# One inference step of a streaming encoder: the last piece of the down projection in the plain form

## The chip, the cores and the metric

The kernel runs on one core of one Trainium2 chip. A core has five engines that run their own instruction streams and meet at semaphores: TensorE (PE, matrix products into PSUM; PEld is its weight load), VectorE (DVE), ScalarE (ACT), GpSimd (POOL, here only issuing DMAs) and SyncE (SP, which issues the other DMAs). The metric is device microseconds of the whole program, the median of repeated runs; lower is better. The weights come from HBM by DMA, everything else is worked on in SBUF (128 partitions) and PSUM (eight banks of 128 x 512 floats).

## The reference

One layer is computed for 384 rows (256 of a new stream, 8 x 16 of running ones). The change lies in the MLP, at its end:

```
hdn = square(relu(rmsnorm(x, g_mlp_pre) @ w_up)) @ w_down     # 2048 -> 8192 -> 2048
x   = x + rmsnorm(hdn, g_mlp_post)
```

All matrices are float32. Ahead of the MLP stand the input projection, a pooling branch, a state-space branch and two output projections; the change does not touch them.

## The kernel before, in words

**Products.** A float32 product is made of three matmuls on operands split in two: a high part `h` (rounded to the PE's fast 32-bit type by ACT, an ACTIVATE with Copy) and a low part `l` (the rest, a DVE subtraction). h·h, h·l and l·h are added up in PSUM. So each weight unit of 128 x 1024 goes through three steps before PE may use it: a 512 KB load on SP's queue into a `w` buffer (`wfetch`, L65), ACT's `wh` (L72), DVE's `wl` (L73). `wpool` has three buffers of each of `w`, `wh`, `wl`; a buffer is handed out again when its last reader is done, so a load waits for an earlier unit's DVE split, and an ACT split waits for PE to be through with an earlier unit.

**Up projection.** `up(f)` makes tile f of 64 (128 of the 8192 hidden columns for all 384 rows) from two weight units, 24 matmuls of 384 columns each, then relu and square (ACT). Two tiles make a pair `R`. `combine(p)` turns pair p into ten 128 x 128 blocks `hh`/`hl`: five raw blocks (H11, H31, H22, H12, H32) and five sums (S1 to S4, H3). The first block of a pair, H21, is used in sums only.

**Down projection.** It runs in eight stretches `c` of 1024 hidden columns, each in two pieces `sb` of 1024 output columns. The first two row blocks (b = 0, 1), the two hidden tiles of a pair and the two 512-column halves of a piece form 2 x 2 blocks and use a seven-product Strassen form; the third row block (b = 2) is done plainly. `blocks(c, sb, w)` runs one piece: eleven groups of twelve matmuls of 512 columns, 132 in all, in the order a, c, b, d, e, f, g. Its weights are four quadrants of 1 MB from `w_dn`, loaded by POOL's queue in `prep`, and three sums of them that DVE makes (`add`, L1312: six halves of 128 x 1024 by the three steps `adds[0]`, `adds[1]`, `adds[2]`), plus one sum inside `blocks`. Every quadrant half is split by ACT (L1345) and DVE (L1346) as above. Products for b = 0, 1 go from PSUM into `acc` by `evict` (L1368); those for b = 2 stay in four banks `c3` until the end.

**Order.** The program is written in one stream; a scheduler places each instruction on its engine by priority and by what is free in its own model. `up(f, steps, steps)` runs its extra steps behind its first and second weight unit; a piece's `adds` are spread over the up tiles that follow its `prep`.

**End.** After `blocks(7, 0)` no up tiles are left: `prep(7, 1)`, its three sums at once, `blocks(7, 1)`. `tally(b, nb, src)` finishes a 512-column block: ACT squares and sums it (L1297), DVE multiplies it by the norm weights `gpo` (L1298); with the fourth block of a row block it makes the norm factor (`postnorm`, L978 to L986, then L1302), scales and adds the residual `x1` (four L1305) and stores (L1308, SP). `x1` (3 MB) and `gpo` (1 MB, scaled by ACT at L1450) are loaded after the last up tile, `x1` by SP, `gpo` by POOL.

Of the kernel before, what the change touches and what calls it, by code (L numbers as in the profile page):

```python
# [6 lines left out]
F32 = mybir.dt.float32  # L7
# [7 lines left out]
P = 128  # L15
# [18 lines left out]
def build(ctx, tc, io):  # L34
# [17 lines left out]
    def mmtile(name):  # L52
        return psm.tile([P, 512], F32, tag="mm", name=name)
# [4 lines left out]
    def behind(ins):  # L58
        return nullcontext() if ins is None else tc.issue_after(ins.ins)
# [1181 lines left out]
    with ExitStack() as mlp:  # L1241
# [25 lines left out]

        HB = {}

        def combine(p):  # L1270
# [21 lines left out]
        def tally(b, nb, src):  # L1292
            dst = end["z"][:, blk(nb)] if b == 2 else acc[:, b, blk(nb)]
            q = end["pool"].tile([P, 512], F32, tag="q3", name=f"q3_{nb}_{b}", bufs=2)
            i = count[b]
            count[b] += 1
            s.activation(q, src, AF.Square, scale=rr[:, b : b + 1], accum_out=end["st"][:, b, i : i + 1])  # L1297
            v.tensor_tensor(dst, src, end["gpo"][:, blk(nb)], ALU.mult)  # L1298
            if i < 3:
                return  # L1300
            y = postnorm(end["pool"], end["st"], b, "n3", doubled=True)
            v.tensor_tensor(y, y, rr[:, b : b + 1], ALU.mult)  # L1302
            for i in range(4):
                z = end["z"][:, blk(i)] if b == 2 else acc[:, b, blk(i)]
                v.scalar_tensor_tensor(  # L1305
                    out=z, in0=z, scalar=y, in1=end["x1"][:, b, blk(i)], op0=ALU.mult, op1=ALU.add
                )
                sy.dma_start(io["y"][b][:, blk(i)], z)  # L1308

        def add(out, a, b):  # L1310
# [276 lines left out]
```

## Time and profile before

| what | us |
|---|---|
| median of 3 runs (lowest, highest) | 2640.62 (2639.19, 2641.0) |
| the profiled execution's own time | 2640.17 |
| its span on the core | 2638.3 |
| PE busy, share of the span | 2607.0, 99% |
| DVE busy, share | 1791.4, 68% |
| ACT busy, share | 1308.0, 50% |

The span counts from the first to the last recorded instruction; 1.87 us lie around it. Rows of a timeline read: start, time, engine, line, operation, what is written and read, shape, and in brackets how long the engine stood idle before it and what ended that. A PE row's time reaches into the next one's, since matmuls are pipelined; what counts is the distance of two starts.

### The profile page before, as it was taken

How to read it: one execution, taken by the hardware profiler on the slowest of the kernel's cores; microseconds unless marked ns; L12 is line 12 of the kernel's file. 1: busy time of each engine (PE TensorE's matmuls, PEld its weight loads, DVE VectorE, ACT ScalarE, POOL GpSimd, SP SyncE). 2: the span in 40 equal slices, each digit the busy share in tenths (PEclk: the TensorE clock that was granted, in tenths of full speed). 3: DMA queues.
4: the chain of work that ended last, by engine and by line, in shares of the span. 5: the costliest groups of instructions: out<-in, count | busy, mean ns of one | idle time of the engine just before them, and what ended most of it. 6: DMA issues, size and time to landing. Idle time of an engine off the chain costs nothing.

```text
span 2638.3 us, 40306 instructions
## 1 busy us (share of the span) xinstructions
PE 2607.0 (99%) x15987; PEld 2506.8 (95%) x15987; DVE 1791.4 (68%) x2396; ACT 1308.0 (50%) x1983; POOL 186.3 (7%) x265
## 2 busy tenths in 40 slices
PE   9999999999999999999999999999999999999996
PEld 8999999999999999999999988999999999999995
DVE  6576334788887888876444435667686867767688
ACT  6443225566566666644333334655454544545453
POOL 0000000001110111120000000000000000000000
PEclk9999999999999999999999999999999999999998
DMA  7444445566666676666655455534344444434342
GB/s 275 141 139 152 146 148 205 185 201 207 231 210 220 205 235 199 233 209 233 193 164 161 153 189 180 184 129 143 128 153 159 144 137 144 143 128 144 128 168 96
DMA packets 138844, 457.76 MB, mean 174 GB/s; under 512 B 17504, under 2 KB 44704, under 8 KB 124704
## 3 DMA queue, kind: packets, MB, share of 16 engines
q1 hardware_dynamic: 116400, 325.93, 38.4%
q0 software_dynamic: 22256, 129.26, 13.4%
q8 instruction: 126, 2.06, 0.3%
q14 instruction: 62, 0.51, 0.1%
HBM read 410.26 MB, written 44.86 MB: 173 GB/s over the span
## 4 chain that ended last, share of the span: by engine, by line
PE 93%; issue 2%; DVE 2%; ACT 1%; DMA 1%; POOL 0%; DVEq 0%; POOLq 0%; ACTq 0%
PE pj_up L102 5%; PE pj_up L100 5%; PE pj_up L101 5%; PE pj_x L100 5%; PE pj_x L102 4%; PE pj_x L101 4%; PE pj_sp L101 3%; PE pj_z L102 3%; PE pj_z L101 3%; PE pj_z L100 3%; PE pj_sp L102 3%; PE pj_sp L100 3%; PE c L1360 2%; PE c L1361 2%; PE c L1359 2%
## 5 line engine op out<-in xcount | busy, mean ns | idle before, releaser
L102 PE MATMUL pj_up<-x1h,wl_up 128*128 128x384 f32 (+1 forms) x1024 | 333.8, 326 | 2.5 <-DVE wl_up L73 2.5
L100 PE MATMUL pj_up<-x1h,wh_up 128*128 128x384 f32 (+1 forms) x1024 | 333.9, 326 | 0.0
L101 PE MATMUL pj_up<-x1l,wh_up 128*128 128x384 f32 (+1 forms) x1024 | 333.7, 326 | 0.0
L100 PE MATMUL pj_x<-xgh,wh_x 128*128 128x384 f32 x768 | 252.0, 328 | 0.0
L102 PE MATMUL pj_x<-xgh,wl_x 128*128 128x384 f32 x768 | 250.6, 326 | 1.3 <-DVE wl_x L73 1.3
L101 PE MATMUL pj_x<-xgl,wh_x 128*128 128x384 f32 x768 | 250.4, 326 | 0.0
L72 ACT ACTIVATE wh_up<-w_up 128x1024 fp32r<-128x1024 f32 x126 | 133.1, 1056 | 189.3 <-PE pj_up L101 113.8
L102 PEld LDWEIGHTS pj_up<-x1h,wl_up 128*128 128x128 f32 x1024 | 193.5, 189 | 2.8 <-DVE wl_up L73 2.8
L73 DVE TENSOR_TENSOR wl_up<-w_up,wh_up 128x1024 fp32r<-128x1024 f32 x126 | 153.7, 1220 | 61.3 <-ACT wh_up L72 60.4
L101 PEld LDWEIGHTS pj_up<-x1l,wh_up 128*128 128x128 f32 x1024 | 193.5, 189 | 0.4
L100 PEld LDWEIGHTS pj_up<-x1h,wh_up 128*128 128x128 f32 x1024 | 193.5, 189 | 0.4
L101 PE MATMUL pj_z<-xgl,wh_z 128*128 128x384 f32 x512 | 166.9, 326 | 0.0
L102 PE MATMUL pj_z<-xgh,wl_z 128*128 128x384 f32 x512 | 166.9, 326 | 0.0
L100 PE MATMUL pj_sp<-abh,wh_sp 128*128 128x384 f32 x512 | 166.9, 326 | 0.0
L101 PE MATMUL pj_sp<-abl,wh_sp 128*128 128x384 f32 x512 | 166.9, 326 | 0.0
L102 PE MATMUL pj_sp<-abh,wl_sp 128*128 128x384 f32 x512 | 166.9, 326 | 0.0
L100 PE MATMUL pj_z<-xgh,wh_z 128*128 128x384 f32 x512 | 166.9, 326 | 0.0
L73 DVE TENSOR_TENSOR wl_sp<-w_sp,wh_sp 128x1024 fp32r<-128x1024 f32 x64 | 78.3, 1223 | 116.6 <-ACT wh_sp L72 116.6
L72 ACT ACTIVATE wh_x<-w_x 128x1024 fp32r<-128x1024 f32 x96 | 101.0, 1052 | 107.0 <-PE pj_z L101 53.0
L73 DVE TENSOR_TENSOR wl_x<-w_x,wh_x 128x1024 fp32r<-128x1024 f32 x96 | 117.3, 1222 | 52.3 <-ACT wh_x L72 52.3
L72 ACT ACTIVATE wh_sp<-w_sp 128x1024 fp32r<-128x1024 f32 x64 | 67.7, 1058 | 166.4 <-PE pj_sp L101 158.3
L100 PEld LDWEIGHTS pj_x<-xgh,wh_x 128*128 128x128 f32 x768 | 145.1, 189 | 2.6 <-issue 0.4
(409 smaller groups left out, 7133.9 us busy)
## 6 DMA issues: line engine op xcount, KB each, us to landing
w_up<-w_up SPq DMA_DIRECT2D x128, 512.0 KB, 3.5
w<-w_dn POOLq DMA_DIRECT2D x64, 1024.0 KB, 5.2
w_x<-w_in SPq DMA_DIRECT2D x96, 512.0 KB, 3.8
w_z<-w_in SPq DMA_DIRECT2D x64, 512.0 KB, 3.6
w_sp<-w_ssd SPq DMA_DIRECT2D x64, 512.0 KB, 3.5
w_ga<-w_ga SPq DMA_DIRECT2D x32, 512.0 KB, 3.5
w_pp<-w_pp SPq DMA_DIRECT2D x32, 512.0 KB, 3.5
hs<-ssm POOLq DMA_DIRECT2D x16, 1024.0 KB, 6.6
```

The source lines that it names most:

```text
L72: cut[0] = s.activation(h, w, AF.Copy)
L73: cut[1] = v.tensor_tensor(l, w, h.bitcast(F32), ALU.subtract)
L100: te.matmul(out, wh, xh, start=first, stop=False, **how)
L101: te.matmul(out, wh, xl, start=False, stop=False, **how)
L102: return te.matmul(out, wl, xh, start=False, stop=last, **how)
L1359: te.matmul(o, h[:, t], vh, start=go, stop=False, skip_group_check=True)
L1360: te.matmul(o, h[:, t], vl, start=False, stop=False, skip_group_check=True)
L1361: last[0] = te.matmul(o, l[:, t], vh, start=False, stop=False, skip_group_check=True)
```

## The change

**1.** The last piece (c = 7, sb = 1) is no longer `prep` and `blocks`. It is done plainly in two passes of 512 columns (nb = 2, 3), with all three row blocks, from a new input `w_tail` that holds these weights as eight units of 128 x 1024 (`kp` = 0 to 3 for each pass). Pass 2 runs unit by unit, 18 matmuls a unit. Pass 3 first has its four units split and kept (two in `wpool`, two in `t1` and `t2`, no longer needed for sums), and then runs row block by row block, 24 matmuls each, so that b = 0 and b = 1 are finished while b = 2 is still multiplied. The plain form needs H21: `combine` of the last four pairs also splits it, into a `w` buffer `h21` that is kept to the end. `tally` adds the finished PSUM block to `acc` (`add=True`) where before `evict` did.

**2.** At the start of the MLP the three `adds` of the first piece each run one up tile later.

**3.** The very last block (b = 2, nb = 3) is not multiplied by `gpo` ahead of the norm factor: when the factor is known, one instruction scales it out of PSUM by both, and one adds the residual.

**4.** `x1` is loaded on POOL's queue, behind `gpo`.

```
-        up(3, (), (adds[0],))
+        up(3)
         combine(1)
-        up(4, (adds[1],), (adds[2],))
-        up(5)
+        up(4, (), (adds[0],))
+        up(5, (adds[1],), (adds[2],))
...
-            sy.dma_start(x1[:, b, :], x1_scr[b])
+            gp.dma_start(x1[:, b, :], x1_scr[b])
         blocks(NC - 1, 0, w)
-        w, *adds = prep(NC - 1, 1)
-        for step in adds:
-            step()
-        blocks(NC - 1, 1, w)
+        for nb in (2, 3):
...
+            if nb == 2:
+                for kp in range(4):
+                    hl = wload(units[kp], names[kp])
+                    with behind(last[0]):
+                        for i in (2 * kp, 2 * kp + 1):
+                            for b in range(3):
+                                mm(b, hl, i)
+                for b in range(3):
+                    tally(b, nb, o[b], b < 2)
+                continue
+            w = []
+            for kp in range(4):
+                f_, name = wfetch(units[kp], names[kp])
+                if kp < 2:
+                    w.append(wsplit((f_, name)))
+                    continue
+                t = pr.tile([P, 2048], F32R, tag=f"t{kp - 1}", name=f"e_{name}")
+                h, l = t[:, :1024], t[:, 1024:]
+                s.activation(h, f_, AF.Copy)
+                v.tensor_tensor(l, f_, h.bitcast(F32), ALU.subtract)
+                w.append((h, l))
+            for b in range(3):
+                with behind(last[0]):
+                    for i in range(8):
+                        mm(b, w[i // 2], i)
+                tally(b, nb, o[b], b < 2)
```

In `tally` and `combine`:

```
+            if add:
+                v.tensor_tensor(dst, dst, src, ALU.add)
...
-            v.tensor_tensor(dst, src, end["gpo"][:, blk(nb)], ALU.mult)
+            g = end["gpo"][:, blk(nb)]
+            if i < 3 or b < 2:
+                v.tensor_tensor(dst, src, g, ALU.mult)
...
+                if b == 2 and i == nb:
+                    v.scalar_tensor_tensor(out=z, in0=src, scalar=y, in1=g, op0=ALU.mult, op1=ALU.mult)
+                    v.tensor_tensor(z, z, x, ALU.add)
...
+            if p < 4 * NC - 4:
+                return
+            if not extra:
+                extra.append(wpool.tile([P, 1024], F32R, tag="w", name="h21"))
+            i = p % 4 * 256
+            eh, el = extra[0][:, i : i + P], extra[0][:, i + P : i + 256]
+            s.activation(eh, R[:, :P], AF.Copy)
+            v.tensor_tensor(el, R[:, :P], eh.bitcast(F32), ALU.subtract)
```

**Where instructions move.** First place: DVE at the start of the MLP, in up tiles 4 and 5 (units 17029 and 17061 are tile 4, 17097 and 17127 tile 5; `t` and `w` rows are the sums, `hl` and `S` rows belong to `combine(1)`). Before:

```order
L73 TENSOR_TENSOR wl_up_0_17032<-w_up_0_17029,wh_up_0_17031 128x1024
L1312 TENSOR_TENSOR t_0_0_16950<-w_0_0_16942,w_0_0_16943 128x1024 x2
L73 TENSOR_TENSOR wl_up_1_17064<-w_up_1_17061,wh_up_1_17063 128x1024
L1312 TENSOR_TENSOR w_0_0_16943<-w_0_0_16943,w_0_0_16945 128x1024 x2
L1312 TENSOR_TENSOR t_0_0_16951<-t_0_0_16950,w_0_0_16945 128x1024 x2
L1277 TENSOR_TENSOR hl_17018<-R_16920,hh_17017 128x640
L1280 TENSOR_TENSOR S_17019<-R_16920 128x128
L1282 TENSOR_TENSOR S_17019<-R_16920 128x256
L1281 TENSOR_TENSOR S_17019<-S_17019,R_16920 128x128
L73 TENSOR_TENSOR wl_up_0_17100<-w_up_0_17097,wh_up_0_17099 128x1024
```

Now (tile 4 is 17027 and 17057, tile 5 is 17093 and 17125):

```order
L73 TENSOR_TENSOR wl_up_1_17060<-w_up_1_17057,wh_up_1_17059 128x1024
L1330 TENSOR_TENSOR t_0_0_16950<-w_0_0_16942,w_0_0_16943 128x1024 x2
L73 TENSOR_TENSOR wl_up_0_17096<-w_up_0_17093,wh_up_0_17095 128x1024
L1282 TENSOR_TENSOR S_17017<-R_16920 128x128
L1284 TENSOR_TENSOR S_17017<-R_16920 128x256
L1279 TENSOR_TENSOR hl_17016<-R_16920,hh_17015 128x640
L1283 TENSOR_TENSOR S_17017<-S_17017,R_16920 128x128
L1330 TENSOR_TENSOR w_0_0_16943<-w_0_0_16943,w_0_0_16945 128x1024
L1285 TENSOR_TENSOR S_17017<-S_17017,R_16920 128x128
L1330 TENSOR_TENSOR w_0_0_16943<-w_0_0_16943,w_0_0_16945 128x1024
L1287 TENSOR_TENSOR hl_17016<-S_17017,hh_17015 128x640
L73 TENSOR_TENSOR wl_up_1_17128<-w_up_1_17125,wh_up_1_17127 128x1024
```

The low part of tile 5's first unit stood behind all three sums and most of `combine(1)`; now it stands behind the first sum alone, and the second sum stands ahead of the low part of tile 5's second unit.

Second place: DVE at the handover from `blocks(7, 0)` to the last piece (`wl_g` is the last split of `blocks(7, 0)`, `Y_0` and `X_0` are its PSUM results). Before:

```order
L1346 TENSOR_TENSOR wl_g_0_1_24415<-t_7_0_23891,wh_g_0_1_24414 128x1024
L1312 TENSOR_TENSOR t_7_1_24436<-w_7_1_24428,w_7_1_24429 128x1024
L1298 TENSOR_TENSOR z_24205<-c_1_16928,gpo_24202 128x512
L1368 TENSOR_TENSOR acc<-acc,Y_0_24211 128x512
L1312 TENSOR_TENSOR t_7_1_24436<-w_7_1_24428,w_7_1_24429 128x1024
L1312 TENSOR_TENSOR w_7_1_24429<-w_7_1_24429,w_7_1_24431 128x1024
L1298 TENSOR_TENSOR acc<-acc,gpo_24202 128x512
L1368 TENSOR_TENSOR acc<-acc,X_0_24210 128x512
L1312 TENSOR_TENSOR w_7_1_24429<-w_7_1_24429,w_7_1_24431 128x1024
L1298 TENSOR_TENSOR acc<-acc,gpo_24202 128x512
L1312 TENSOR_TENSOR t_7_1_24437<-t_7_1_24436,w_7_1_24431 128x1024 x2
L1346 TENSOR_TENSOR wl_a_1_0_24448<-w_7_1_24428,wh_a_1_0_24447 128x1024
```

Now:

```order
L1364 TENSOR_TENSOR wl_g_0_1_24424<-t_7_0_23891,wh_g_0_1_24423 128x1024
L73 TENSOR_TENSOR wl_wt_0_24442<-w_wt_0_24439,wh_wt_0_24441 128x1024
L1313 TENSOR_TENSOR z_24214<-c_1_16928,gpo_24211 128x512
L1386 TENSOR_TENSOR acc<-acc,Y_0_24220 128x512
L73 TENSOR_TENSOR wl_wt_1_24466<-w_wt_1_24463,wh_wt_1_24465 128x1024
L1313 TENSOR_TENSOR acc<-acc,gpo_24211 128x512
L1386 TENSOR_TENSOR acc<-acc,X_0_24219 128x512
L73 TENSOR_TENSOR wl_wt_2_24490<-w_wt_2_24487,wh_wt_2_24489 128x1024
```

The six sum halves that stood between `wl_g` and the last piece's first low part are gone; the first unit's low part follows `wl_g` directly.

Third place: ACT in the last piece (`q_2_0` to `q_2_2` square the three blocks of pass 2, `e_wt_2` and `e_wt_3` are the high parts of the third and fourth unit of pass 3). Before, at the end of the last piece:

```order
L1345 ACTIVATE wh_g_1_1_24690<-t_7_1_24437 128x1024
L1297 ACTIVATE q_3_0_24596,st_24206<-acc,rr 128x512
L1297 ACTIVATE q_3_2_24631,st_24206<-c_3_16930,rr 128x512
L981 ACTIVATE n_n_24636<-st_24206,n_n_24634 128x1
L1297 ACTIVATE q_3_1_24656,st_24206<-acc,rr 128x512
L981 ACTIVATE n_n_24661<-st_24206,n_n_24659 128x1
L1297 ACTIVATE q_2_0_24701,st_24206<-acc,rr 128x512
L981 ACTIVATE n_n_24706<-st_24206,n_n_24704 128x1
```

Now:

```order
L1519 ACTIVATE e_wt_2_24562<-w_wt_2_24560 128x1024
L1310 ACTIVATE q_2_0_24536,st_24215<-acc,rr 128x512
L1310 ACTIVATE q_2_1_24540,st_24215<-acc,rr 128x512
L1310 ACTIVATE q_2_2_24543,st_24215<-c_2_16929,rr 128x512
L1519 ACTIVATE e_wt_3_24567<-w_wt_3_24565 128x1024
L1310 ACTIVATE q_3_0_24595,st_24215<-acc,rr 128x512
L981 ACTIVATE n_n_24600<-st_24215,n_n_24598 128x1
L1310 ACTIVATE q_3_1_24644,st_24215<-acc,rr 128x512
L981 ACTIVATE n_n_24649<-st_24215,n_n_24647 128x1
L1310 ACTIVATE q_3_2_24692,st_24215<-c_3_16930,rr 128x512
L981 ACTIVATE n_n_24696<-st_24215,n_n_24694 128x1
```

Before, three norm factors were made behind the last split, the last one for row block 0; now the third row block's comes last, and the high part of the fourth kept unit stands behind the three squares of pass 2.

More of the change, by code (lines that the diff above doesn't have):

```diff
@@ L1268, in build @@
         HB = {}
+        extra = []
         def combine(p):
@@ L1290, in build, with tally @@
         end = {}
-        def tally(b, nb, src):
+        def tally(b, nb, src, add=False):
             dst = end["z"][:, blk(nb)] if b == 2 else acc[:, b, blk(nb)]
+            if add:
+                v.tensor_tensor(dst, dst, src, ALU.add)
+                src = dst
             q = end["pool"].tile([P, 512], F32, tag="q3", name=f"q3_{nb}_{b}", bufs=2)
@@ L1304, in tally @@
                 z = end["z"][:, blk(i)] if b == 2 else acc[:, b, blk(i)]
-                v.scalar_tensor_tensor(
-                    out=z, in0=z, scalar=y, in1=end["x1"][:, b, blk(i)], op0=ALU.mult, op1=ALU.add
-                )
+                x = end["x1"][:, b, blk(i)]
+                if b == 2 and i == nb:
+                    v.scalar_tensor_tensor(out=z, in0=src, scalar=y, in1=g, op0=ALU.mult, op1=ALU.mult)
+                    v.tensor_tensor(z, z, x, ALU.add)
+                else:
+                    v.scalar_tensor_tensor(out=z, in0=z, scalar=y, in1=x, op0=ALU.mult, op1=ALU.add)
                 sy.dma_start(io["y"][b][:, blk(i)], z)
@@ new lines, in build, with mm @@
+        for nb in (2, 3):
+            o = [mmtile(f"wt{nb}_{b}") if nb == 2 else psd.tile([P, 512], F32, tag="XY"[b], name=f"wt{nb}_{b}") for b in range(2)]
+            o.append(c3[nb])
+            def mm(b, hl, i):
+                wh, wl = hl
+                mh, ml = lhs(i)[b]
+                q = slice(i % 2 * 512, i % 2 * 512 + 512)
+                out, vh, vl = pairs(o[b]), woven(wh[:, q]), woven(wl[:, q])
+                te.matmul(out, mh, vh, start=i == 0 and b < 2, stop=False, skip_group_check=True)
+                te.matmul(out, mh, vl, start=False, stop=False, skip_group_check=True)
+                last[0] = te.matmul(out, ml, vh, start=False, stop=False, skip_group_check=True)
+            names = [f"wt{nb}_{kp}" for kp in range(4)]
+            units = [io["w_tail"][nb - 2, kp] for kp in range(4)]
+            if nb == 2:
[24 more added lines that the diff above has]
+                tally(b, nb, o[b], b < 2)
@@ L1547 @@
         ).reshape(8, 2, 4, P, 2048),
+        "w_tail": _moving(np, a["w_down"][0][7168:, 1024:]),
         "state_pool": np.ascontiguousarray(a["state_pool"][0].reshape(NB, 15, KD, P).transpose(3, 2, 0, 1)),
```

5 lines of the change are left out of this document (added).

## The prediction

> **What bounds the kernel now.** I read the page first, then PE's waits from the last part of the program, then the stretches around them. On the page PE works for nearly the whole span; only the last of the forty slices is thin.
>
> ```profile
> span 2638.3 us, 40306 instructions
> ...
> PE 2607.0 (99%) x15987; PEld 2506.8 (95%) x15987; DVE 1791.4 (68%) x2396; ACT 1308.0 (50%) x1983; POOL 186.3 (7%) x265
> ...
> PE   9999999999999999999999999999999999999996
> ```
>
> So time can be won only where PE waits, or behind its last matmul. PE's waits from 1664 us to the end (engine and line that waited, what for, us, times, longest) are five:
>
> ```profile
> PE X L1360 <- DVE wl_a L1346: 4.7, 1, 4.7
> PE pj_up L102 <- DVE wl_up L73: 2.5, 1, 2.5
> PE c L1360 <- DVE wl_e L1346: 2.3, 3, 0.8
> PE c L1359 <- ACT wh_a L1345: 1.2, 1, 1.2
> PE X L1359 <- DVE acc L1368: 0.9, 1, 0.9
> ```
>
> The second is at the start of the MLP, the others in the last 60 us. Those I cut into four: the handover to the last piece, its first matmuls, the rest of them, and what follows the last matmul (bounds; length; busy time of PE, PEld, DVE, ACT, POOL with counts; granted clock; DMA share, GB/s).
>
> ```profile
> 2583.30:2591.20 7.90, 1.16 (x3) 0.37 (x2) 7.58 (x9) 3.10 (x6) 0.00 (x0) 0.74 0.00 0
> 2591.20:2597.40 6.20, 6.16 (x15) 4.91 (x16) 3.95 (x7) 1.06 (x1) 0.00 (x0) 0.51 0.00 0
> 2597.40:2624.00 26.60, 25.68 (x117) 21.53 (x115) 21.86 (x35) 13.44 (x21) 0.00 (x0) 1.00 0.00 1
> 2624.00:2638.30 14.30, 0.01 (x1) 0.00 (x0) 10.60 (x24) 1.11 (x3) 0.00 (x0) 0.64 0.59 220
> ```
>
> For 7.9 us PE does three matmuls while DVE is full; then fifteen run at a clock of 0.51; then it is full; then DVE alone works 10.6 of 14.3 us.
>
> **The sums one up tile later.** The early stall, on DVE and PE:
>
> ```profile
> 1684.56 1.22 DVE L73 TENSOR_TENSOR wl_up<-w_up,wh_up 128x1024 fp32r<-128x1024 f32 x1
> 1686.54 2.36 DVE L1312 TENSOR_TENSOR w<-w,w 128x1024 f32<-128x1024 f32 x2 [0.76 <-DVE wl_up L73]
> 1688.82 2.35 DVE L1312 TENSOR_TENSOR t<-t,w 128x1024 f32<-128x1024 f32 x2
> 1692.57 1.21 DVE L73 TENSOR_TENSOR wl_up<-w_up,wh_up 128x1024 fp32r<-128x1024 f32 x1
> ...
> 1693.83 0.43 PE L102 MATMUL pj_up<-x1h,wl_up 128*128 128x384 f32 x1 [2.47 <-DVE wl_up L73]
> ...
> 1694.00:1697.00 3.00, 3.00 (x19) 3.00 (x20) 2.98 (x3) 2.58 (x4) 0.00 (x0) 1.00 0.60 179
> ```
>
> Tile 5's first low part (1692.57) stands behind two sums of 4.7 us, and PE loses 2.47 us. In the new order it stands behind the first sum alone, and ends near 1684.56 + 2.35 + 1.2, about 1688, three us before PE asks at 1691.36. Who is late next? The second unit's low part, behind `combine(1)` and the second sum. Its high part comes at
>
> ```profile
> 1690.29 1.07 ACT L72 ACTIVATE wh_up<-w_up 128x1024 fp32r<-128x1024 f32 x1 [4.42 <-DMA w_up<-w_up]
> ```
>
> so its low part, after the high and low part of `combine`'s 640 columns (5/8 of the 1.06 and 1.22 us that 1024 take in the rows further down, 1.4) and its own 1.22, ends near 1694. PE would ask at 1691.36 plus 24 matmuls of 384 columns (3/4 of the 0.216 us step found below, 3.9), so 1695.3. I take -2.5; bounds 0 and -2.5, since a load 1.3 us later would open the wait again at this unit.
>
> **The gpo load.** In `blocks(7, 0)` ACT waits for `gpo`, which shares the DMA engines with the three `x1` loads issued just before it:
>
> ```profile
> 2560.62 1.91 ACT L1450 ACTIVATE gpo<-gpo 128x2048 f32<-128x2048 f32 x1 [2.05 <-DMA gpo<-g_mlp_post]
> ...
> 2565.62 0.38 PE L1359 MATMUL X<-wh_d,hh 128*128 128x512 f32 x1
> ...
> 2568.18 1.22 DVE L1346 TENSOR_TENSOR wl_e<-w,wh_e 128x1024 fp32r<-128x1024 f32 x1
> ...
> 2606.85 0.38 PE L1359 MATMUL X<-wh_d,hh 128*128 128x512 f32 x1
> ...
> 2608.70 1.21 DVE L1346 TENSOR_TENSOR wl_e<-w,wh_e 128x1024 fp32r<-128x1024 f32 x1
> ```
>
> Behind `gpo` on POOL's queue, `x1` no longer delays it; it has to land 7.9 us after its issue instead of 9.9, and 1 MB takes 5.2 at the median (last row quoted below), so the 2.05 us should go. The splits d and e then follow sooner: in the last piece, which has no `gpo`, `wl_e` starts 1.85 us after the first d matmul, in `blocks(7, 0)` 2.56 us after it, and PE waits for `wl_e` in both. Gain 0.7; bounds 0 and -1.0. `x1` itself is read some 50 us after its issue, so its own place costs nothing.
>
> **The last piece.** PE's rows at its ends, and a run of 52 rows, 51 steps, without a wait:
>
> ```profile
> 2583.11 0.38 PE L1361 MATMUL X<-wh_g,hl 128*128 128x512 f32 x1
> ...
> 2591.24 0.79 PE L1360 MATMUL X<-wl_a,hh 128*128 128x512 f32 x1 [4.66 <-DVE wl_a L1346]
> ...
> 2612.62 0.38 PE L1361 MATMUL c<-wh_e,hl 128*128 128x512 f32 x1
> ...
> 2623.63 0.38 PE L1361 MATMUL X<-wh_g,hl 128*128 128x512 f32 x1
> ```
>
> A step is 11.01 / 51 = 0.216 us. Without waits the 132 matmuls would start from 2583.33 and the last one 28.3 us later, at 2611.6. It starts at 2623.63, 12.0 us late: 7.5 from the handover (7.9 less two matmuls), 3.1 from the slow clock (the 6.2 us stretch above at about half rate), the last 1.4 mostly from `wl_e`.
>
> The plain form adds twelve matmuls: +2.6 us. It takes away the six sum halves and the 1 MB quadrant they wait for, so the handover depends on unit 0 alone. Is that early? With `h21` in a `w` buffer two buffers are left. Units 0 and 1 take those of the last up tile, whose last split starts at 2542.35; with 3.4 us for a load both lie in SBUF by 2547, 36 us ahead. ACT's split of unit 0 needs the `wh` buffer of group f's first half, which PE leaves 24 matmuls, 5.2 us, before the end of `blocks(7, 0)`, and DVE's stands right behind `wl_g`
>
> ```profile
> w_up<-w_up SPq DMA_DIRECT2D x18, 512.0 KB, 3.4
> ...
> 2542.35 1.22 DVE L73 TENSOR_TENSOR wl_up<-w_up,wh_up 128x1024 fp32r<-128x1024 f32 x1
> ...
> 2578.53 1.22 DVE L1346 TENSOR_TENSOR wl_g<-t,wh_g 128x1024 fp32r<-128x1024 f32 x1
> ...
> L72 ACT ACTIVATE wh_up<-w_up 128x1024 fp32r<-128x1024 f32 x126 | 133.1, 1056 | 189.3 <-PE pj_up L101 113.8
> L73 DVE TENSOR_TENSOR wl_up<-w_up,wh_up 128x1024 fp32r<-128x1024 f32 x126 | 153.7, 1220 | 61.3 <-ACT wh_up L72 60.4
> ```
>
> so it ends near 2580.9, 2.4 us before PE needs it. No gap, so no slow clock either: -7.5 and -3.1. A wait of 2.47 us leaves the clock whole: it is 1.00 in the stretch from 1694 quoted above.
>
> From the second unit on, two buffers make a chain: load 3.4, high part 1.06, low part 1.22, some 5.7 us per two units, while PE spends 7.8 us on two (36 x 0.216). It fits, in the last three up tiles too, where the new `h21` takes its buffer; `combine`'s eight splits of 128 columns (an eighth of 1.06 and of 1.22 each) lie there under PE's 99%. The one place where it doesn't is the last unit. Counted from the first matmul (0): pass 2 ends at 15.5, and pass 3 asks for its fourth unit 18 matmuls later, at 19.4. The third unit takes the buffer of pass 3's first, whose split waits until PE leaves pass 2's second unit at 7.8 and ends at 10.2; load to 13.6, high part, low part: 15.9. The fourth is loaded by 17.6 in the same way. But behind the third low part DVE adds blocks 0 and 1 to `acc` (0.6 to 0.7 each), and ACT squares three blocks ahead of the fourth high part:
>
> ```profile
> 2619.74 0.38 PE L1361 MATMUL c<-wh_f,hl 128*128 128x512 f32 x1
> ...
> 2620.22 0.69 ACT L1297 ACTIVATE q<-c,rr 128x512 f32<-128x512 f32 x1 [1.99 <-PE c L1361]
> 2621.03 0.29 ACT L981 ACTIVATE n_n<-st,n_n 128x1 f32<-128x1 f32 x1
> ...
> 2621.03 0.69 DVE L1298 TENSOR_TENSOR z<-c,gpo 128x512 f32<-128x512 f32 x1 [0.26 <-ACT q L1297]
> ...
> 2631.22 0.15 DVE L983 RECIPROCAL n_n<-n_n 128x1 f32<-128x1 f32 x1
> ...
> 2632.11 2.74 DVE L1305 SCALAR_TENSOR_TENSOR acc<-acc,n_n,x1r 128x512 f32<-128x512 f32 x4
> ```
>
> Three squares of 0.7 from 16.6 end at 18.7, the high part at 19.7, the low part (behind a 0.7 multiply and small norm steps) at 21.1. PE loses 1.5 us there; bounds 0 (a scheduling slack I misjudge) and 4 (loads as slow as 5 us). The last piece so changes by +2.6 - 7.5 - 3.1 - 1.4 + 1.5 = -7.9.
>
> **Behind the last matmul.** Now 14.7 us (2623.63 to 2638.3): DVE finishes three row blocks one after another. In the new order two are finished under row block 2's 24 matmuls (5.2 us; row block 1's add, square, factor and four scalings, 0.7 + 0.9 + 1.3 + 2.74, end about 6 us after its last matmul, before row block 2's factor is there). What is left: square 0.48 after the last matmul's start, factor input at +1.29 (2619.74 to 2621.03), +0.29 root, +0.89 to the scaling (2631.22 to 2632.11), together +2.5; three scalings of 0.69; one out of PSUM, which no row shows: it has the two kinds of operand of the L1298 and L1305 rows, both 0.69, so I take 0.7, with bounds of that and twice that; one add of 0.7; then the last store and the end, 3.45 us as now (2634.85 to 2638.3). Sum 2.5 + 2.1 + 0.7 + 0.7 + 3.45 = 9.4, so -5.3; bounds -4 and -6.
>
> **Sum.** -2.5 - 0.7 - 7.9 - 5.3 = -16.4. From the profiled execution's 2640.17: 2623.8. The runs' median is 0.45 above that execution, so I say 2624.
>
> **Rivals.** (a) The early stall stays or moves to the second unit: 2626.5. For it: the margin of 1.1 us; against it: three us of room at the first. (b) A cold handover: unit 0's split comes late, as `wl_a` does now, and PE restarts at half clock: up to +7.5 + 3.1, so 2634.6. For it: ACT and DVE are full there, and f's `wh` buffer is freed late; against: 2.4 us of room. By the Trainium skill ("TensorE: Matmul & The Clock Gate", Part 1) the clock halves after an idle window of about 3.4 us and returns after as long a busy one; the trace agrees that 2.47 us of waiting is harmless and 7.9 us is not, but here 6.1 us ran slow, so the page would price the slow part at 1.7 us, not 3.1. (c) Slower: the two-buffer chain of loads. If a tail load takes L, two units take L + 2.3 against PE's 7.8; six units lose 3 x (L - 5.5). The change loses from L = 11 on. The longest weight load of this program is
>
> ```profile
> DMA to landing us min/median/max: 4.9/5.2/16.3
> ```
>
> (quadrants, four at once); L = 16.3 gives 2624 + 32 = 2656. Against it: the DMA engines carry nothing in the last piece now (0.00 above), and its loads are 4 MB in 40 us. (d) The plain form only shifts the work, and nothing is won: 2640.
>
> **How the numbers follow.** Forecast 0.72, (a) 0.12, (b) 0.10, (c) 0.03, (d) 0.03. A change is told from none at 0.2%, 5.3 us. Forecast, (a) and most of (b) are faster by more: 0.92; the rest of (b) and (d) 0.05; (c) 0.03. The sum's own bounds reach from 2621.5 (no wait at the fourth unit, all of the `gpo` wait, the short end) to 2629 (a wait of 4, the early stall kept); with one us more below, and a part of (b) above: 2620.5 to 2632.
>
> **What would show it.** Right: no wait of `pj_up` on `wl_up` near 1691; PE steps of 0.216 straight over the handover with the clock at 1.00; a wait of 1 to 2 us before the fourth unit of pass 3; about 9.4 us from the last matmul to the end. Wrong: a wait on `wl_wt` at a unit's start, a slow clock in the tail, or the tail's end set by row block 1 or by the loads of `x1`.

## The result

The changed kernel takes 2623.63 us (median of four runs, 2623.38 to 2624.44), the kernel before beside it 2640.81 us (2639.19 to 2643.35): a ratio of 0.9938, with a 95% interval of 0.9925 to 0.995. That is 17.2 us less; the forecast was 2624, from a sum of -16.4 us. Two executions of the kernel before, taken beside the experiments, ran for 7127 and 15537 us; they count as slow and are in none of the ratios and ranges below. The profiled execution took 2624.44 us, with a span of 2622.7 us against 2638.3.

### The profile page after: what moved, and what is told of

Its sections match the earlier page's. It is cut to its first block, busy times and chain, and to the rows that moved or that the text cites. A ratio compares the mean times of both kernels' runs of the same rounds, so it can differ in the third digit from the quotient of the medians.

```text
span 2622.7 us, 40313 instructions
## 1 busy us (share of the span) xinstructions
PE 2606.7 (99%) x15999; PEld 2508.9 (96%) x15999; DVE 1775.3 (68%) x2383; ACT 1302.9 (50%) x1981; POOL 185.8 (7%) x264
## 4 chain that ended last, share of the span: by engine, by line
PE 96%; DVE 2%; ACT 1%; issue 1%; DMA 1%; POOL 0%; ACTq 0%; POOLq 0%; DVEq 0%
PE pj_up L100 6%; PE pj_up L102 6%; PE pj_up L101 6%; PE pj_x L100 4%; PE pj_x L102 4%; PE pj_x L101 4%; PE pj_z L100 3%; PE pj_z L101 3%; PE pj_sp L102 3%; PE pj_sp L101 3%; PE pj_sp L100 3%; PE pj_z L102 3%; PE c L1378 2%; PE c L1379 2%; PE X L1378 2%; PE X L1379 2%
```

## The profile after

The page of the changed kernel begins with its span and the busy time of the engines. PE is busy for as long as before (2606.7 and 2607.0 us, with twelve matmuls more and fewer of them slow), in a span that is 15.6 us shorter; DVE has 16 us less to do.

```profile
span 2622.7 us, 40313 instructions
...
PE 2606.7 (99%) x15999; PEld 2508.9 (96%) x15999; DVE 1775.3 (68%) x2383; ACT 1302.9 (50%) x1981; POOL 185.8 (7%) x264
```

PE's waits from 1664 us on (engine, line, what for: us in total, times, longest) were five kinds and 11.6 us before. Now 1.9 us are left. `pj_up` for `wl_up`, `X` for `wl_a` and for `acc`, and `c` for `wh_a` are gone, and of three waits for `wl_e` one is left.

```profile
PE wt L1496 <- DVE e_wt L1520: 0.8, 1, 0.8
PE c L1378 <- DVE wl_e L1364: 0.8, 1, 0.8
PE wt L1495 <- ACT e_wt L1519: 0.3, 1, 0.3
```

**Early.** DVE's instructions around the sums (start, us, line, tiles). Tile 5's first low part now ends at 1688.3; it ended at 1693.8 before. The second one stands behind the second sum and ends at 1695.1, and PE waits for neither.

```profile
1684.81 2.35 DVE L1330 TENSOR_TENSOR t<-w,w 128x1024 f32<-128x1024 f32 x2
1687.08 1.22 DVE L73 TENSOR_TENSOR wl_up<-w_up,wh_up 128x1024 fp32r<-128x1024 f32 x1
...
1693.85 1.22 DVE L73 TENSOR_TENSOR wl_up<-w_up,wh_up 128x1024 fp32r<-128x1024 f32 x1
```

**Late.** PE's instructions from the last matmul of `blocks(7, 0)`, whose start is the first row, to the last of all. The handover is one step of 0.21 us; the two rows with a bracket are the fourth unit of pass 3.

```profile
2580.63 0.38 PE L1379 MATMUL X<-wh_g,hl 128*128 128x512 f32 x1
2580.84 0.38 PE L1495 MATMUL wt<-wh_wt,h 128*128 128x512 f32 x1
...
2600.74 0.48 PE L1495 MATMUL wt<-e_wt,h 128*128 128x512 f32 x1 [0.30 <-ACT e_wt L1519]
...
2602.05 0.48 PE L1496 MATMUL wt<-e_wt,h 128*128 128x512 f32 x1 [0.83 <-DVE e_wt L1520]
...
2613.38 0.38 PE L1497 MATMUL c<-e_wt,hl 128*128 128x512 f32 x1
```

The stretches that answer to the four shown of before (bounds; length; busy time of PE, PEld, DVE, ACT, POOL; clock; DMA share, GB/s): PE is full and its clock whole over the handover, and the stretch behind the last matmul is 9.2 us, not 14.3.

```profile
2570.00:2580.00 10.00, 10.00 (x48) 8.74 (x48) 10.00 (x12) 6.14 (x9) 0.00 (x0) 1.00 0.04 7
2580.00:2590.00 10.00, 10.00 (x48) 8.77 (x47) 5.32 (x10) 4.37 (x7) 0.00 (x0) 1.00 0.62 199
2596.00:2602.00 6.00, 4.92 (x22) 3.73 (x20) 5.68 (x13) 3.14 (x7) 0.00 (x0) 1.00 0.26 87
2613.50:2622.70 9.20, 0.26 (x2) 0.00 (x0) 5.97 (x13) 1.07 (x3) 0.00 (x0) 0.75 0.61 228
```

DVE in that last stretch: row block 1's four scalings, row block 2's factor (from L982), three scalings, the result out of PSUM (L1322) and its add.

```profile
2612.52 2.74 DVE L1325 SCALAR_TENSOR_TENSOR acc<-acc,n_n,x1r 128x512 f32<-128x512 f32 x4
2615.17 0.21 DVE L982 TENSOR_SCALAR n_n<-st,n_n 128x1 f32<-128x1 f32 x1
...
2616.18 2.07 DVE L1325 SCALAR_TENSOR_TENSOR z<-z,n_n,x1r 128x512 f32<-128x512 f32 x3
2618.18 0.74 DVE L1322 SCALAR_TENSOR_TENSOR z<-c,n_n,gpo 128x512 f32<-128x512 f32 x1
2618.95 0.69 DVE L1323 TENSOR_TENSOR z<-z,x1r 128x512 f32<-128x512 f32 x1
```

## The experiments

Medians move by some us from run to run, for a reason that the last section shows. So each profile is also cut at five marks: the start of the matmul behind the wait for `pbuf` near 64 us (t1), of the first d and the last g matmul of `blocks(7, 0)` (d, g), of the last matmul, and the end. The table gives the times between them, differences of starts in the trace, and whether the clock was halved right behind t1. The last column is good to 0.05 us, since the spans that it uses are given to a tenth.

| kernel | t1 | clock there | t1 to d | d to g | g to last | last to end |
|---|---|---|---|---|---|---|
| before | 63.50 | half | 2502.12 | 17.49 | 40.52 | 14.67 |
| after | 65.17 | half | 2498.68 | 16.78 | 32.75 | 9.32 |
| after, again | 63.59 | full | 2497.19 | 16.78 | 32.81 | 9.33 |
| before, sums later | 64.51 | full | 2497.26 | 17.41 | 40.44 | 14.68 |
| before, x1 on POOL | 64.23 | half | 2502.00 | 16.77 | 39.44 | 14.36 |
| plain piece alone | 64.92 | full | 2500.02 | 17.35 | 32.89 | 9.62 |
| after, sums early | 64.78 | full | 2500.15 | 16.78 | 32.86 | 9.33 |
| after, no scaling out of PSUM | 65.33 | half | 2498.73 | 16.77 | 32.91 | 9.26 |
| after, fourth unit ahead | 64.40 | full | 2497.01 | 16.78 | 31.67 | 9.64 |
| the same, again | 63.51 | full | 2497.45 | 16.78 | 31.48 | 9.58 |
| after, unit by unit | 64.80 | full | 2497.42 | 16.78 | 31.08 | 15.52 |
| after, late load | 64.84 | full | 2497.51 | 16.77 | 44.58 | 8.90 |
| after, late split | 64.91 | half | 2498.83 | 16.77 | 39.77 | 9.32 |
| after, loads doubled | 65.27 | half | 2498.79 | 16.78 | 41.92 | 9.34 |

My theory was the prediction's sum: four gains in four places that don't touch each other. The rivals were a stall that only moves (a), a cold handover (b), and loads that come late (c).

### The sums alone

```diff
-        up(3, (), (adds[0],))
+        up(3)
         combine(1)
-        up(4, (adds[1],), (adds[2],))
-        up(5)
+        up(4, (), (adds[0],))
+        up(5, (adds[1],), (adds[2],))
```

> The kernel before, with the sums of the first piece's weights put one up tile later and nothing else changed. My theory: the 2.5 us that PE waits for wl_up near 1691 go and come back nowhere, since the first unit of tile 5 has three us of room and the second one about one us; -2.5, so about 2638.2 where the kernel before takes 2640.7, and no wait of pj_up on wl_up over 0.3 us after 1670. Rival (a): the stall moves to the second unit of tile 5 or to the first piece's first blocks, and the time is that of the kernel before, 2640.7.

It takes 2636.54 us, 3.3 less than the kernel before beside it (2639.85): ratio 0.999, interval 0.998 to 0.9999. Of the time, that is just outside no change; the trace is plain. Between 1664 us and the handover, PE waits for `wl_e` alone:

```profile
PE c L1360 <- DVE wl_e L1346: 1.5, 2, 0.8
```

The reverse, the changed kernel with its sums early:

> The changed kernel with its first edit alone undone: the sums of the first piece's weights stand at their old up tiles again. My theory: the wait of 2.5 us for wl_up near 1691 is back and nothing else moves; +2.5 against the changed kernel on the same chip, and up to +4 in executions in which the clock falls behind that wait. Rival (a): the stall costs less, since units that wait there would wait elsewhere; less than +1.

It takes 2625.63 us, 2.66 more than the changed kernel on the same chip (2622.97). The stall is back in one place:

```profile
PE pj_up L102 <- DVE wl_up L73: 2.5, 1, 2.5
```

From t1 to d, the six profiles with the sums late and a full clock take 2497.01 to 2497.51 (mean 2497.31), the two with the sums early 2500.02 and 2500.15 (mean 2500.09): 2.8 us. Rival (a) is out. Most of the 0.3 beyond the recorded wait lies in how it is counted: in the kernel with its sums early, the matmul that waits starts 2.80 us behind the one ahead of it (1690.35 to 1693.15), 2.64 more than a step of 0.16, and the next step takes 0.1 longer.

### x1 behind gpo, alone

```diff
-            sy.dma_start(x1[:, b, :], x1_scr[b])
+            gp.dma_start(x1[:, b, :], x1_scr[b])
```

> The kernel before, with the three loads of x1 issued on POOL's queue behind gpo instead of on SP's just before it; nothing else. My theory: gpo lands about 5 us after its issue instead of 9.9, ACT's wait of 2.05 us for it goes, and blocks(7, 0) gets 0.7 us shorter. But the four quadrants of the last piece are issued on POOL behind x1 here, so the handover may be later than it was; at most -0.7 (2640.0), and with the quadrants later by some us up to +3 (2643). Rival: the late gpo cost PE nothing and the time does not change, 2640.7; then blocks(7, 0) is still 17.5 us from its first d matmul to its last g matmul.

2638.24 us, 1.6 less than before; the ratio 0.9994 (0.9985 to 1.0004) tells nothing. The trace does. ACT's copy of `gpo` has no wait any more:

```profile
2559.09 1.89 ACT L1450 ACTIVATE gpo<-gpo 128x2048 f32<-128x2048 f32 x1
```

`gpo` lands 4.8 us after its issue instead of 9.9, and d to g is 16.77 instead of 17.49: -0.72. The column splits cleanly: 17.35 to 17.49 in the three kernels with `x1` on SP, 16.77 or 16.78 in the eleven others. The quadrants were not late: the handover's waits are those of before within 0.2 us each. That g to last is 1.1 us shorter too is the clock's: the slow stretch behind the handover lasts 3.6 us here, not 6.1.

### The plain piece alone

The diff is the change without its other three edits.

> The changed kernel with three parts undone: the sums stand at their old up tiles, x1 is loaded on SP's queue, and the very last result is copied out of PSUM by its multiply as before. What is left is the plain last piece with its kept units. My theory: it carries -7.9 (handover, slow clock, twelve more matmuls, one wait) and nearly all of the -5.3 behind the last matmul, and the wait of 2.5 us near 1691 and the late gpo are back; so -13.2, about 2627.5 where the kernel before takes 2640.7. Rival: the last piece carries all of the change and the other parts nothing, 2623.8.

2626.33 us, 13.5 less than before; ratio 0.9951 (0.9934 to 0.9968). Expected were -13.2. In the table the two gains stand in the two last columns: 32.89 for 40.52, and 9.62 for 14.67. The early stall (2.3) and the late `gpo` (two waits for `wl_e`, 1.5) are back:

```profile
PE pj_up L102 <- DVE wl_up L73: 2.3, 1, 2.3
PE c L1373 <- DVE wl_e L1359: 1.5, 2, 0.8
```

### The very last result through SBUF again

```diff
-            g = end["gpo"][:, blk(nb)]
-            if i < 3 or b < 2:
-                v.tensor_tensor(dst, src, g, ALU.mult)
+            v.tensor_tensor(dst, src, end["gpo"][:, blk(nb)], ALU.mult)
...
-                if b == 2 and i == nb:
-                    v.scalar_tensor_tensor(out=z, in0=src, scalar=y, in1=g, op0=ALU.mult, op1=ALU.mult)
-                    v.tensor_tensor(z, z, x, ALU.add)
-                else:
-                    v.scalar_tensor_tensor(out=z, in0=z, scalar=y, in1=x, op0=ALU.mult, op1=ALU.add)
+                v.scalar_tensor_tensor(
+                    out=z, in0=z, scalar=y, in1=end["x1"][:, b, blk(i)], op0=ALU.mult, op1=ALU.add
+                )
```

> The changed kernel with the very last result multiplied by gpo into SBUF first, and then scaled like the other three blocks, as the kernel before does it. My theory: behind the last matmul DVE is full with row block 1's scalings until row block 2's factor is ready, so one multiply of 0.7 us there stands against the one add of 0.7 us that the changed form needs at the end; the time is that of the changed kernel, 2623.6, within 0.3. Rival: DVE has time for the multiply before the factor is ready, and the form out of PSUM costs the add; then this kernel is 0.7 us faster, 2622.9. Second rival: the multiply delays the factor, and it is 0.7 us slower, 2624.3.

2622.36 us, 17.5 below the kernel before on its chip, where the changed kernel is 17.2 below on its own; the last column is 9.26 against 9.32, the same within its rounding. The scaling out of PSUM buys nothing: it saves a multiply ahead and pays an add behind, and DVE has no gap between the two.

### Pass 3 unit by unit

```diff
-            for b in range(3):
-                with behind(last[0]):
-                    for i in range(8):
+            with behind(last[0]):
+                for i in range(8):
+                    for b in range(3):
                         mm(b, w[i // 2], i)
+            for b in range(3):
                 tally(b, nb, o[b], b < 2)
```

> The changed kernel with pass 3 run unit by unit, as pass 2 is, instead of row block by row block, so that no unit has to be kept and the three row blocks end together. My theory: the 5.3 us won behind the last matmul come from the row blocks ending one after another, two of them under row block 2's 24 matmuls; here the stretch behind the last matmul is again about 14 to 15 us instead of 9.3, and the wait of 1.1 us at the fourth unit goes, since PE comes to it 8 us later; together +4, about 2627.6 where the changed kernel takes 2623.6. Rival: the stretch is set by the last result alone (square, factor, four scalings, store), whatever the order of the row blocks; then the time stays within 1 us of 2623.6 or falls by the wait.

2627.29 us, 3.7 more than the changed kernel. Behind the last matmul it is 15.5 us again, of which DVE works 12.1 (columns as above):

```profile
2600.00:2610.10 10.10, 10.10 (x49) 8.83 (x47) 1.39 (x3) 0.11 (x1) 0.00 (x0) 1.00 0.00 0
2610.10:2625.60 15.50, 0.36 (x2) 0.00 (x0) 12.10 (x31) 2.74 (x9) 0.00 (x0) 0.62 0.55 203
```

So the gain behind the last matmul comes from the order of the row blocks, as the prediction had it: here DVE works 1.39 us in the ten before the last matmul, and has the three finishes all behind it. The 144 steps take 31.08 us, 0.2158 each: without the wait at the fourth unit, the last piece has none.

### The fourth unit ahead of pass 2's sums

```diff
-                for b in range(3):
-                    tally(b, nb, o[b], b < 2)
+                o2 = o
                 continue
...
-                s.activation(h, f_, AF.Copy)
+                act4 = s.activation(h, f_, AF.Copy)
                 v.tensor_tensor(l, f_, h.bitcast(F32), ALU.subtract)
                 w.append((h, l))
+            for b in range(3):
+                with behind(act4):
+                    tally(b, 2, o2[b], b < 2)
```

> The changed kernel with the split of the last piece's fourth unit of the second block written ahead of pass 2's squares and sums, and those squares held back on ACT until the split is done. My theory: that unit is late (PE waits 0.3 us for its high part and 0.8 for its low part) only because the split stands behind pass 2's squares and sums on ACT and DVE; written ahead of them it is there in time, the waits go to 0.3 us or less together, and the time falls by about 1.3 us, to 2622.3 where the changed kernel takes 2623.6. Rival (c): what is late is the load itself, because units alternate between two buffers; then the waits stay where they are, now as waits of ACT on the DMA, and the time stays at 2623.6 or gets longer by the later squares.

2621.40 us; ratio to before 0.9928 (0.9912 to 0.9945). The fourth high part is taken at 2596.16, after a wait for its load, and PE keeps one wait of 0.3 us:

```profile
2596.16 1.06 ACT L1518 ACTIVATE e_wt<-w_wt 128x1024 fp32r<-128x1024 f32 x1 [2.74 <-DMA w_wt<-w_tail]
...
2598.53 0.48 PE L1496 MATMUL wt<-e_wt,h 128*128 128x512 f32 x1 [0.32 <-DVE e_wt L1519]
```

In the changed kernel the unit was late because of what stood ahead of it on ACT and DVE: ACT took it at 2599.64, while its load, issued at 2595.04, was there about 1.2 us earlier (an estimate with the median of 3.4 us that these loads take). On one chip with the changed kernel:

> The kernel with the fourth unit's split ahead of pass 2's squares and sums once more, now beside the changed kernel on the same chip. In the profiles the 1.1 us of waits at the fourth unit shrink to 0.3 and the last piece is 1.1 us shorter, and the stretch behind the last matmul is 0.3 longer: so -0.8 against the changed kernel. Rival: the 2.2 us between the two medians of the earlier runs are all due to this edit; -2.2.

2623.04 us against 2622.97: no difference in the time. From g to the end the trace has 41.06 and 41.31 us against 42.07 and 42.14, so 0.8 to 1.1 less, and that is lost in a spread of 3.4 us; in the second profile PE does not wait for the fourth unit at all. The 2.2 us between the earlier medians were not this edit. It is the shortest form I have, by the trace alone.

### A late handover, made on purpose

First the load of unit 0 waits for the last result of `blocks(7, 0)`, by a small copy into its buffer:

```diff
-                    hl = wload(units[kp], names[kp])
+                    if kp == 0:
+                        f_ = wpool.tile([P, 1024], F32, tag="w", name="w_late")
+                        v.tensor_copy(f_[:, :8], acc[:, 0, :8])
+                        sy.dma_start(f_, units[0])
...
```

> The changed kernel with one artificial dependence: the load of the last piece's first unit waits until the last result of blocks(7, 0) is there. All results are computed as before. My theory of the handover: a gap of some 8 us between the last matmul of blocks(7, 0) and the first of the last piece, and behind it about 6 us at half clock, that is 3 us more; so +11, about 2634.6 where the changed kernel takes 2623.6, with the granted clock near 0.5 for about 6 us. Rival: the slow clock in the kernel before was not made by the gap but by how sparse the matmuls behind it were (waits for wl_e); then the clock stays at 1.00 and the time is only +8, 2631.6. By the Trainium skill ("TensorE: Matmul & The Clock Gate", Part 1) the slow stretch would last about 3.4 us and cost 1.7; a sentence that changes neither number above.

2634.27 us, 10.6 more; ratio to before 0.9976 (0.9967 to 0.9986). The total came out as expected by luck, for its parts did not. The gap is 7.3 us, and the clock is at half behind it, but for 3.3 us, not 6:

```profile
2579.50:2586.70 7.20, 0.00 (x1) 0.00 (x0) 1.66 (x6) 1.84 (x4) 0.00 (x0) 0.76 0.20 73
2586.70:2590.00 3.30, 3.18 (x7) 2.10 (x8) 2.36 (x2) 0.98 (x2) 0.00 (x0) 0.50 0.23 62
```

The rest was lost at the fourth unit, where two waits of 1.26 and 0.83 us put the clock to half a second time. In the slow stretch PE was busy for 3.18 of 3.30 us, so it isn't sparse matmuls that keep the clock down; rival (b)'s mechanism holds, and the gap makes the clock slow.

Then only the split of unit 0 waits, by a cast of 8 columns from the same result into its `wh` buffer:

```diff
-                    hl = wload(units[kp], names[kp])
+                    f_, name = wfetch(units[kp], names[kp])
+                    if kp == 0:
...
+                        v.tensor_copy(h[:, :8], acc[:, 0, :8])
+                        s.activation(h, f_, AF.Copy)
+                        v.tensor_tensor(l, f_, h.bitcast(F32), ALU.subtract)
```

> The changed kernel with one artificial dependence: the split of the last piece's first unit (not its load) waits until the last result of blocks(7, 0) is there. All results are computed as before. My theory: the gap is a small cast of 0.1 to 0.6 us, a high part of 1.06, a low part of 1.22, about 2.9 us in two parts (the first matmul needs the high part only, the second the low part); a wait of 2.47 us left the clock whole in the kernel before, so this one does too; +2.9, about 2626.5 where the changed kernel takes 2623.6. Rival: the clock falls behind a gap this short as well, and 3 us more are lost; 2629.6.

2631.35 us, 7.7 more; ratio to before 0.9964 (0.9951 to 0.9977). Here the rival was right: a gap of 3.7 us is enough, and the clock stays at half for 5.4 us, longer than behind the gap of 7.3.

```profile
2580.90:2584.60 3.70, 0.00 (x0) 0.00 (x0) 1.67 (x7) 2.82 (x4) 0.00 (x0) 0.83 0.00 0
2584.60:2590.00 5.40, 5.35 (x12) 3.81 (x13) 2.36 (x2) 0.63 (x1) 0.00 (x0) 0.50 0.45 163
```

The gap was also 0.8 longer than I had counted, since the scheduler put unit 1's high part ahead of unit 0's on ACT. In g to last: +3.9 for the gap, start to start and less one step, and +3.0 for twelve steps at half clock (5.63 us instead of 2.59) make 6.9 of the 7.0.

### The loads doubled

```diff
-                    hl = wload(units[kp], names[kp])
+                    f_ = wfetch(units[kp], names[kp])
+                    sy.dma_start(f_[0], units[kp])
+                    hl = wsplit(f_)
...
                 f_, name = wfetch(units[kp], names[kp])
+                sy.dma_start(f_, units[kp])
```

> The changed kernel with every unit of the last piece loaded twice in a row into its buffer, so that a load takes some 6.8 us instead of 3.4. This is rival (c) with its price. By the prediction's formula, 3 x (L - 5.5), six units lose 3.9 us. A closer count, which I hold likelier: the loss does not gather evenly, since pass 3 asks for four units within 3.9 us of its first matmul. The units come in pairs L + 2.3 = 9.1 us apart, so the fourth is ready some 7.7 us after PE asks for it, against 1.1 to 1.7 us now; +6.3, all of it at the third and fourth unit of pass 3, with waits of ACT on the DMA. If the two loads of a unit overlap, so that L is only 5, the loss is 1 us or less.

2633.93 us, 11.0 more than the changed kernel beside it. PE's waits in the last piece:

```profile
PE wt L1495 <- ACT e_wt L1522: 5.4, 1, 5.4
PE wt L1496 <- DVE wl_wt L73: 1.5, 2, 0.8
PE wt L1496 <- DVE e_wt L1523: 0.5, 1, 0.5
PE wt L1495 <- ACT wh_wt L72: 0.5, 1, 0.5
```

Together 7.9 us, against 1.2 there without the doubling, all in pass 3: 2.0 at its first two units, 5.9 at the third, none at the fourth. The closer count had +6.3, at the third and fourth, and it is +6.7; that is partly luck, since the loads took more than the 6.8 us that it went by. From the first issue to the start of ACT's split, which waited for the load in each of six units, it was 6.9 to 8.1 us, 7.7 in the mean (3.4 and 3.6 in the two units of the changed kernel where ACT waits for the load). With 7.7 the prediction's formula gives 6.6. But the wait of 5.4 is followed by some 4 us at half clock, and g to last grows by 9.2. (The 1.8 us by which the medians differ more are of the size of the clock's draw at t1.) So rival (c) has a working mechanism, and a higher price than its formula gives, by the clock.

### The changed kernel once more

> The changed kernel once more, for the spread of its time and as the base for the three others on the same chip. In the ten profiles so far a wait of 2.65 us near 62 us (PE for pbuf, the same in all of them) was followed by a clock of one half for 2.4 to 3 us in five and by a full clock in the other five, which is worth 1.2 to 2 us of the time. My theory of the spread: the changed kernel has no other wait long enough, so its runs fall in two groups some 1.5 to 2.5 us apart, between 2621.5 and 2624.5, while the kernel before, which also restarts at the handover, spreads over 5 us or more. Rival: the spread has nothing to do with the clock, and both kernels spread alike.

Median 2622.97 us, ratio 0.9934 (0.9921 to 0.9947); its five runs lie between 2621.45 and 2624.92, those of the kernel before on the same chip between 2637.82 and 2644.42. The spread is half as wide (of five runs against fourteen). Whether it falls in two groups five runs don't tell: three at 2621.45 to 2622.97 with a mean clock of 0.999, and two at 2624.43 and 2624.92 with 0.998.

## Why the prediction was right

By the table, after against before in the two profiled executions:

- **Early sums**, -2.5 predicted: t1 to d is 3.4 shorter, both with the slow clock behind t1; with a full clock it is 2.8. PE waits for neither unit of tile 5, as counted.
- **gpo**, -0.7 predicted: -0.71.
- **Last piece**, -7.9 predicted: -7.77. The parts hold too: from g, 144 steps of 0.2157 us are 31.06, so 1.69 us are lost at the fourth unit (1.5 predicted), and before 132 steps were 28.47 of 40.52, 12.05 lost (12.0).
- **Behind the last matmul**, -5.3 predicted: -5.35. Here two deviations cancel by luck. Row block 1's scalings still hold DVE when the steps to row block 2's factor could begin: they end at 2615.26, the factor's first step starts at 2615.17, and its input was there at 2614.89. So row block 2's scalings start 2.8 us after the last matmul's start, not 2.5; and store and end take 3.06, not 3.45. The scaling out of PSUM, which the prediction could only put between 0.7 and 1.4, takes 0.744 us; the same operation on SBUF alone takes 0.746.
- These sum to -17.3 in the profiles, of which 1.7 are hidden there by a later t1 (65.17 against 63.50). The changed kernel's other profile has its t1 at 63.59, so that is none of the change. In the medians the two kernels are 17.2 apart.

Three statements of the prediction were wrong, though none changed the sum. "A wait of 2.47 us leaves the clock whole" holds in the four profiles that have this wait, but not as a rule: a wait of 2.65 us is followed by either clock, and that the 2.47 us were harmless was luck (both below). The slow stretch's price of 3.1 us is one draw of several. And rival (c)'s formula, 3 x (L - 5.5), spread the loss over six units, where pass 3 in truth asks for four units within 3.9 us; it also left out the clock: 9.2 us were lost at a load of 7.7 us, where it gives 6.6. Its break-even, a load of 11 us, is not refuted: a line through both points (no loss at 3.5 us, 9.2 at 7.7) reaches the gain of 16.4 at about 11 as well, an estimate from these two runs. The scaling out of PSUM, priced as a mere exchange ahead of its run, was one: the gain of 5.3 is all of the row blocks' order.

## What to carry to other kernels

Before a faster algorithm is used for the last piece of a product, ask what it needs ahead of its first matmul and what it leaves behind its last: 12 matmuls fewer saved 2.6 us here, and cost 7.5 of gap and 3.1 of slow clock at the handover. Let row blocks end one after another, not together, where each has a long finish on another engine. Price an idle PE with the clock behind it, which is one to three us more and differs from run to run with the place of the wait in the clock's periods (below); and where medians move by as much, cut the traces at common marks and compare stretch by stretch.

## What the runs showed of the hardware

**The same wait, two clocks.** Near 64 us PE waits 2.64 or 2.65 us for `pbuf` in all fourteen profiles. In six the clock is at half behind it, in eight it stays full. The changed kernel has both. In its first profile, matmuls of 384 columns start 0.32 us apart until 68.18:

```profile
65.17 0.66 PE L100 MATMUL pj_ga<-xgh,wh_ga 128*128 128x384 f32 x1 [2.64 <-DVE pbuf L381]
65.62 0.53 PE L101 MATMUL pj_ga<-xgl,wh_ga 128*128 128x384 f32 x1
...
67.86 0.53 PE L102 MATMUL pj_ga<-xgh,wl_ga 128*128 128x384 f32 x1
68.18 0.38 PE L100 MATMUL pj_ga<-xgh,wh_ga 128*128 128x384 f32 x1
```

In its second they are 0.16 us apart from the start:

```profile
63.59 0.40 PE L100 MATMUL pj_ga<-xgh,wh_ga 128*128 128x384 f32 x1 [2.65 <-DVE pbuf L381]
63.82 0.33 PE L101 MATMUL pj_ga<-xgl,wh_ga 128*128 128x384 f32 x1
63.99 0.33 PE L102 MATMUL pj_ga<-xgh,wl_ga 128*128 128x384 f32 x1
```

That is worth 1.5 us (2498.68 and 2497.19 from t1 to d). The start of the program, whose first matmuls also run slow, puts t1 itself anywhere from 63.50 to 65.33. Together that is up to 3.3 us from one execution to the next, enough for medians of four or five runs to differ by 2.

**When the clock falls and comes back.** In the kernel before, the matmuls behind this wait start at the full clock, and slow down in the middle of a dense run, 1.1 us later:

```profile
63.50 0.40 PE L100 MATMUL pj_ga<-xgh,wh_ga 128*128 128x384 f32 x1 [2.65 <-DVE pbuf L381]
...
64.39 0.33 PE L102 MATMUL pj_ga<-xgh,wl_ga 128*128 128x384 f32 x1
64.55 0.45 PE L100 MATMUL pj_ga<-xgh,wh_ga 128*128 128x384 f32 x1
64.79 0.53 PE L101 MATMUL pj_ga<-xgl,wh_ga 128*128 128x384 f32 x1
...
67.67 0.51 PE L101 MATMUL pj_ga<-xgl,wh_ga 128*128 128x384 f32 x1
67.99 0.36 PE L102 MATMUL pj_ga<-xgh,wl_ga 128*128 128x384 f32 x1
68.19 0.33 PE L100 MATMUL pj_ga<-xgh,wh_ga 128*128 128x384 f32 x1
```

It is slow from about 64.6 to about 68.0, 3.4 us. In the kernel with `x1` on POOL it is the same, from 65.6 to 69.0. So what PE did is judged at moments of the clock's own, some 3.4 us apart, and not when PE stops or starts. The granted clock of all fourteen traces bears that out: between 60 us and the last matmul each slow stretch lasts 3.41, 6.82 or 10.24 us, and the edges of one execution lie whole multiples of 3.413 us apart. The Trainium skill ("TensorE: Matmul & The Clock Gate", Part 1) says that: a window of about 3.4 us, free-running, which does not reset with the program. The trace agrees on both. Where the Trainium skill has the clock fall after an idle window, the trace differs: PE worked for at least 0.7 us in any 3.4 around a wait of 2.65, and the clock could fall all the same.

**What is judged is a share of the period.** This was read from the traces afterwards; no run was made to test it. Cut at those moments, the handover of the kernel before reads (columns as above: length, busy time of PE and the others, clock):

```profile
2583.67:2587.08 3.41, 0.97 (x2) 0.37 (x2) 3.41 (x4) 2.73 (x5) 0.00 (x0) 1.00 0.00 0
2587.08:2590.49 3.41, 0.00 (x0) 0.00 (x0) 3.41 (x5) 0.00 (x0) 0.00 (x0) 0.50 0.00 0
2590.50:2593.91 3.41, 2.67 (x6) 2.18 (x7) 3.41 (x4) 0.00 (x0) 0.00 (x0) 0.50 0.00 0
2593.91:2597.32 3.41, 3.41 (x9) 2.69 (x8) 1.16 (x5) 1.06 (x1) 0.00 (x0) 0.50 0.00 0
```

PE is busy for 0.97 us of the period ahead of the fall. Two periods later 2.67 us are not enough to bring the clock back, and one period later 3.41 are. In the fourteen profiles from 55 us on, by the profile's busy time (whose matmul ends are modelled), each full-clock period with PE busy for 1.38 us or less is followed by half clock, and each with 1.65 or more by a full one; of those from 1.42 to 1.64 only one (1.64) is followed by half. A slow period with PE busy for 2.81 us or more is followed by a full clock, one with 2.67 or less is not.

That accounts for the same wait with two clocks: an edge cuts the wait of 2.65 us at another place in each execution. The period that ends in or behind it holds 0.92 to 1.38 us of work in the six profiles whose clock falls (1.08 in the changed kernel's first), and in the eight others no period there holds less than 1.42. The harmless wait of 2.47 us was cut the same way, into two periods with enough work in each:

```profile
1689.38:1692.79 3.41, 1.99 (x13) 1.69 (x11) 3.41 (x7) 1.07 (x1) 0.00 (x0) 1.00 0.04 18
1692.79:1696.20 3.41, 2.37 (x14) 2.37 (x15) 3.41 (x5) 2.15 (x4) 0.00 (x0) 1.00 0.36 95
```

**How long it stays slow** then does not follow from how long PE was idle. Counted from PE's restart to the clock's edge it is 6.1 us behind the handover before (one wait of 4.7, two of about 1 ahead of it), 4.7 and 3.6 in its two variants, 5.5 behind 3.7 us, 3.4 behind 7.3, 3.9 behind 5.4. It follows from where PE restarts. In the late split that is at 2584.61, which leaves 2.10 us of work in the period that ends at 2586.75, not enough, so one more period is slow. In the late load PE restarts at 2586.7, as a period begins, and only that one is slow.
